# The MLP of a decoder block as two sweeps: up-projection by seven products of halves with factors parked in DRAM, then down-projection with two row blocks per accumulation

## The chip, the cores and the metric

The kernel is one program on one core of a Trainium2 chip. A core has TensorE (PE, matrix products from SBUF into PSUM), VectorE (DVE), ScalarE (ACT), GpSimd (POOL) and SyncE (SP), which here issues the DMA transfers between DRAM and SBUF. Each engine works through its own queue in order; semaphores tie the queues together. The metric is the device time of one execution in microseconds (us), as the median of several runs. One execution was recorded by the hardware profiler, and all rows below come from it.

## The reference, cut to what matters

The layer holds an attention-like part (gated DeltaNet beside differential attention), its output projection, and an MLP. The change is in the MLP alone.

```python
S, D_MODEL, D_FF = 512, 2048, 8192
h = h + einsum("bse,ed->bsd", mix, w_o)
u = rms_norm(h, mlp_norm)
hid = square(relu(einsum("bsd,df->bsf", u, w_up)))     # w_up 2048 x 8192
h = h + einsum("bsf,fd->bsd", hid, w_down)             # w_down 8192 x 2048
return rms_norm(h, final_norm)
```

All of it is float32. The kernel makes each float32 product from three products in a shorter format (float32r): every operand is written as hi + lo, and hi·hi, hi·lo and lo·hi are added up in PSUM.

## The kernel before, in words

Weights come in units of 128 partitions x 1024 numbers (512 KB). `load_w` (L160) issues a unit's DMA on SP's queue, each behind the load before it. `parts` splits the unit `raw`: ACT copies it to `hi` (L172), DVE subtracts to get `lo` (L174). `hi` and `lo` have three buffers each (`BUFS`), so unit n can be split only once TensorE is done with unit n−3. `raw` has six buffers. A scheduler decides the order in which the instructions of the streams stand in each engine's queue.

The hidden layer is cut into 16 blocks of 512 columns. Three things are done for a block.

- **Up** (`up_steps`, `cols_steps`): plain products, four groups of 128 hidden columns, each over 16 k tiles of 128, all 512 tokens wide: 4 x 16 x 3 = 192 matmuls of 512 columns. Its weights are the units with tag `x`. ACT makes the squared ReLU. Block 0 (`up_first`) is done first, in the time in which the transposed and normalised u is still being made (`to_feature_major`, `split_rows`, L189).
- **Left factors** (`seven_steps`, `two`): a block's 512 x 512 activations are taken as 2 x 2 blocks a11, a12, a21, a22 of 256 x 256. Winograd's form of Strassen's scheme needs seven left factors: a11, a12, a22 and the sums s1 = a21 + a22, s2 = s1 − a11, s4 = a12 − s2, s3 = a11 − a21. DVE makes the sums (L786 to L797); each factor is split by ACT (L774) and DVE (L775) and stays in SBUF.
- **Down** (`block_steps`, `product`): for each of two pairs p of column groups, the four quarters of the weights b11, b12, b21, b22 (two k tiles by 512 columns) are combined on DVE to t1 to t4 (L838, L844, L852, L858) in place of the loaded quarters, and seven products of 12 matmuls of 512 columns are added by DVE to the rows `h` in SBUF, 16 additions of 128 x 512 (L824 and L826). There are 15 blocks x 2 pairs in this form; block 15 is done by plain products (`plain_steps`).

The down of block b is woven with the up of the blocks after it: after every other product comes a step of up. A plain block costs 8 products of quarters where the scheme has 7.

Of the kernel before, what the change touches and what calls it, by code (L numbers as in the profile page):

```python
# [31 lines left out]
def hybrid_block(ctx: ExitStack, tc: tile.TileContext, x, attn_norm, w_in, conv_w, a_log, dt_bias,  # L32
# [601 lines left out]
    def attn_cols(hd, st):  # L634
        """Columns of q and k of both maps of a head."""
# [20 lines left out]
    def attention(hd, st, vt, keep=None):  # L656
        """The sweep over the query blocks, each in three stages that follow one another a step apart."""
# [110 lines left out]
    def half_tile():  # L768
        """[feature, token half, k tile, token]: two k tiles of a factor."""
        return big("p", [P, 2, 2, 256], nm="hf")  # L770

    def two(src):
        z = big("w", [P, 2, 2, 256], F32R, nm="op")
        A.activation(z[:, 0], src, AF.Copy)  # L774
        V.tensor_sub(z[:, 1], src, z[:, 0].bitcast(F32))  # L775
        return z[:, 0], z[:, 1]

    def seven_steps(left, f):
        """The seven left factors from a block's two K halves, in the order of their use."""
# [6 lines left out]
        V.tensor_add(s1, a21, a22)  # L786
        yield
        f["s1"] = two(s1)
        V.tensor_sub(s2, s1, a11)
        yield  # L790
        f["s2"] = two(s2)
        s4 = s1
        V.tensor_sub(s4, a12, s2)
        yield
        f["s4"] = two(s4)
        s3 = s2
        V.tensor_sub(s3, a11, a21)  # L797
        yield
        f["s3"] = two(s3)
        yield  # L800
        f["a22"] = two(a22)
        yield

    def product(bank, fac, wts, first, last_):
        (ah, al), (bh, bl) = fac, wts
        for k in range(2):
            for t in range(2):
                st = slice(t * P, (t + 1) * P)
                T.matmul(bank[t], lhsT=ah[:, k, st], rhs=bh[:, k, :], start=first and k == 0, stop=False, skip_group_check=True)  # L809
                T.matmul(bank[t], lhsT=ah[:, k, st], rhs=bl[:, k, :], start=False, stop=False, skip_group_check=True)  # L810
# [265 lines left out]
```

## Time and profile before

| what | value |
|---|---|
| median of 3 runs | 2296.26 us (2293.96 to 2299.38) |
| span of the profiled execution | 2291.4 us |
| TensorE busy in the span | 2251.6 us, 10,713 matmuls and transposes |
| VectorE busy | 1499.7 us |
| ScalarE busy | 896.7 us |
| GpSimd busy | 55.8 us |
| DMA, mean over the span | 107 GB/s |

The profiled execution lasted a span of 2291.4 us between its first and last instruction, 4.9 us under the median of the runs; what lies around the span is in that difference. The busy time of an engine is the time in which at least one of its instructions ran. Matmuls are pipelined, so their durations in a row are longer than the distance between their starts. Times in the rows count from the start of the span: about 0 to 960 us is the attention half with its projections, 962 to 1010 us the first block of up, 1010 to 2220 us the woven up and down, and the rest the last block and the final norm.

### The profile page before, as it was taken

Reading aid. Unit: us, or ns where it says so; the run is one execution under the profiler, and the core shown is the slowest. Engines: PE = TensorE matmul, PEld = TensorE weight load, DVE = VectorE, ACT = ScalarE, POOL = GpSimd, SP = SyncE. Lnnn points to the kernel's source line nnn. Section 1 sums busy time; section 2 is a strip of 40 time slices with the busy share of each in tenths; the row PEclk is TensorE's granted clock in tenths of the full one; section 3 lists DMA queues with packets and bytes.
Section 4 is the critical chain, followed back from the end, with each engine's and each line's share of the span. In section 5 each row is a group of like instructions: output and inputs, shape, how many; then the busy total and the mean of one; then the engine's idle time right before and its main releaser. Section 6 shows DMA issues by size and latency. Waiting matters only on the chain.

```text
span 2291.4 us, 27556 instructions
## 1 busy us (share of the span) xinstructions
PE 2251.6 (98%) x10713; PEld 1870.3 (82%) x10713; DVE 1499.7 (65%) x2296; ACT 896.7 (39%) x1468; POOL 55.8 (2%) x85
## 2 busy tenths in 40 slices
PE   6999999999999999999999999999999999999998
PEld 6988778778888788788888888888888888888886
DVE  5356977863255533446777787677777778767776
ACT  5233344432344532443443344334334334334443
POOL 0001101100000000000000000000000000000000
PEclk9999999999999999999999999999999999999999
DMA  5444333334232424332433324233233332323332
GB/s 175 126 115 119 106 108 95 115 88 113 83 88 91 153 83 133 107 101 83 129 92 102 110 83 129 92 120 92 85 127 92 108 104 86 126 92 119 92 129 93
DMA packets 286440, 245.49 MB, mean 107 GB/s; under 512 B 17211, under 2 KB 229478, under 8 KB 286310
## 3 DMA queue, kind: packets, MB, share of 16 engines
q1 hardware_dynamic: 285632, 243.45, 34.7%
q8 instruction: 84, 1.38, 0.2%
q10 hardware_dynamic: 678, 0.28, 0.1%
q14 instruction: 46, 0.38, 0.1%
HBM read 232.66 MB, written 11.03 MB: 106 GB/s over the span
## 4 chain that ended last, share of the span: by engine, by line
PE 93%; DVE 5%; ACT 1%; DMA 1%; issue 0%; POOL 0%; ACTq 0%; POOLq 0%; DVEq 0%
PE s L230 9%; PE s L231 9%; PE s L229 9%; PE acc L810 6%; PE acc L809 6%; PE acc L811 6%; PE acc L229 5%; PE acc L230 5%; PE acc L231 5%; PE acc L245 3%; PE acc L246 3%; PE acc L247 3%; PE s L810 2%; PE s L809 2%; PE s L811 2%; PE s L246 2%
## 5 line engine op out<-in xcount | busy, mean ns | idle before, releaser
L174 DVE TENSOR_TENSOR lo<-raw,hi 128x1024 fp32r<-128x1024 f32 (+2 forms) x370 | 444.1, 1201 | 427.3 <-ACT hi L172 416.6
L172 ACT ACTIVATE hi<-raw 128x1024 fp32r<-128x1024 f32 (+2 forms) x370 | 384.7, 1041 | 682.2 <-PE acc L230 135.8
L229 PE MATMUL s<-u,hi 128*128 128x512 f32 x960 | 373.4, 389 | 0.0
L230 PE MATMUL s<-u,hi 128*128 128x512 f32 x960 | 373.4, 389 | 0.0
L231 PE MATMUL s<-u,lo 128*128 128x512 f32 x960 | 373.4, 389 | 0.0
L174 DVE TENSOR_TENSOR lo<-x,hi 128x1024 fp32r<-128x1024 f32 x120 | 146.8, 1223 | 181.1 <-ACT hi L172 181.1
L229 PE MATMUL acc<-u,hi 128*128 128x512 f32 x640 | 259.8, 406 | 0.5 <-DVE dvl L653 0.5
L230 PE MATMUL acc<-u,hi 128*128 128x512 f32 x640 | 251.5, 393 | 0.0
L172 ACT ACTIVATE hi<-x 128x1024 fp32r<-128x1024 f32 x120 | 127.5, 1062 | 315.1 <-PE s L230 226.3
L231 PE MATMUL acc<-u,lo 128*128 128x512 f32 x640 | 250.2, 391 | 0.0
L810 PE MATMUL acc<-lo,op 128*128 128x512 f32 x600 | 233.4, 389 | 0.0
L811 PE MATMUL acc<-hi,op 128*128 128x512 f32 x600 | 233.4, 389 | 0.0
L809 PE MATMUL acc<-hi,op 128*128 128x512 f32 x600 | 233.1, 389 | 0.0
L824 DVE TENSOR_TENSOR h<-acc,h 128x512 f32<-128x512 f32 x360 | 232.2, 685 | 0.6 <-PE acc L811 0.5
L229 PEld LDWEIGHTS s<-u,hi 128*128 128x128 f32 x960 | 180.2, 188 | 37.4
L231 PEld LDWEIGHTS s<-u,lo 128*128 128x128 f32 x960 | 180.2, 188 | 37.4
L230 PEld LDWEIGHTS s<-u,hi 128*128 128x128 f32 x960 | 180.2, 188 | 37.4
L245 PE MATMUL acc<-hi,u 128*128 128x512 f32 (+2 forms) x384 | 145.3, 378 | 3.0 <-DVE cv L391 1.8
L247 PE MATMUL acc<-hi,u 128*128 128x512 f32 (+2 forms) x384 | 140.8, 367 | 0.0
L231 PEld LDWEIGHTS acc<-u,lo 128*128 128x128 f32 x640 | 120.2, 188 | 25.2
L229 PEld LDWEIGHTS acc<-u,hi 128*128 128x128 f32 x640 | 120.4, 188 | 24.9 <-issue 0.9
L246 PE MATMUL acc<-lo,u 128*128 128x512 f32 (+2 forms) x384 | 140.4, 366 | 0.0
(261 smaller groups left out, 3230.9 us busy)
## 6 DMA issues: line engine op xcount, KB each, us to landing
raw<-in_w_down_dram SPq DMA_DIRECT2D x128, 512.0 KB, 5.4
x<-in_w_up_dram SPq DMA_DIRECT2D x120, 512.0 KB, 4.6
raw<-in_w_in_dram SPq DMA_DIRECT2D x96, 512.0 KB, 3.9
raw<-in_w_o_dram SPq DMA_DIRECT2D x32, 512.0 KB, 4.2
raw<-in_w_in_dram SPq DMA_DIRECT2D x16, 384.0 KB, 3.9
x<-in_x_dram SPq DMA_DIRECT2D x8, 512.0 KB, 5.0
raw<-in_x_dram SPq DMA_DIRECT2D x8, 512.0 KB, 4.0
raw<-in_w_up_dram SPq DMA_DIRECT2D x8, 512.0 KB, 3.9
```

The source lines that it names most:

```text
L172: A.activation(hi, raw, AF.Copy)
L174: floor["lo"] = V.tensor_sub(lo, raw, hi.bitcast(F32))
L229: T.matmul(po, lhsT=hi[:, j, :], rhs=ah, start=k == 0, stop=False)
L230: T.matmul(po, lhsT=hi[:, j, :], rhs=al, start=False, stop=False)
L231: T.matmul(po, lhsT=lo[:, j, :], rhs=ah, start=False, stop=k == KD - 1)
L245: T.matmul(o, lhsT=ah[:, st], rhs=bh, start=k == 0, stop=False)
L246: T.matmul(o, lhsT=ah[:, st], rhs=bl, start=False, stop=False)
L247: T.matmul(o, lhsT=al[:, st], rhs=bh, start=False, stop=k == KD - 1)
L809: T.matmul(bank[t], lhsT=ah[:, k, st], rhs=bh[:, k, :], start=first and k == 0, stop=False, skip_group_check=True)
L810: T.matmul(bank[t], lhsT=ah[:, k, st], rhs=bl[:, k, :], start=False, stop=False, skip_group_check=True)
L811: T.matmul(bank[t], lhsT=al[:, k, st], rhs=bh[:, k, :], start=False, stop=last_ and k == 1, skip_group_check=True)
L824: V.tensor_add(dst, bank[t], dst)
```

## The change

The MLP runs as two sweeps instead of one woven stream.

**Up sweep.** Block 0 stays plain. For blocks 1 to 15 the up-projection is done by the seven products as well, with the transposed u as one factor: 2 x 2 blocks of 1024 k by 256 tokens. `u_factors` makes the seven factors of u once and keeps them in SBUF; for this u is first put together again as hi + lo, 16 additions of 128 x 512 on GpSimd (`uf`). Per block `up_steps` loads eight weight units of four k tiles x 256 columns, makes t1 to t4 on DVE (eight subtractions of 128 x 1024, L1081), and `up_product` runs seven products of two units, 24 matmuls of 256 columns per unit. DVE adds the products up from PSUM (L1109, L1122, L1128, L1129), GpSimd makes c22 (L1131). While block b is computed, `seven_steps` makes the left factors of block b − 1: the four sums now on GpSimd (L790, L793, L798, L803), the splits on ACT (L771) and DVE (L772), and `keep` stores each factor to DRAM (`fscr`, L781) on SP's queue. The rows h are stored to DRAM (`hscr`) to make room, and come back (`hb`) for the second sweep.

**Down sweep.** Fourteen blocks go in seven groups of two: the product of one factor pair of both blocks is accumulated in the same PSUM banks, so the 16 additions to the rows come once for two blocks. `recall` (L818) loads the left factors from DRAM. t1 and t2 are made on DVE, t3 and t4 on GpSimd (L854), two subtractions of 128 x 1024 for each. Block 14 is a group by itself, block 15 plain. Its left factors are stored at the beginning of the sweep. Buffers for `raw` are nine instead of six. The scratch memory of the DMA machinery is cut to 1024 bytes, and comments are removed.

```diff
-    BUFS = {"p": 10, "x": 2, "w": 8, "m": 2, "u": 16, "raw": 6, "hi": 3, "lo": 3}
+    BUFS = {"p": 10, "x": 2, "w": 8, "m": 2, "u": 16, "raw": 9, "hi": 3, "lo": 3}
...
+    def keep(b, name, src):
+        z = pair_of(src, "w")
+        fscr[b, name] = dp.tile([P, 1024], F32, name=f"f_{name}_{b}")
+        nc.sync.dma_start(out=fscr[b, name], in_=z.bitcast(F32).rearrange("p a k s -> p (a k s)"))
...
+        G.tensor_add(s1, a21, a22)
+        keep(b, "a11", a11)
+        yield
+        G.tensor_sub(s2, s1, a11)
+        keep(b, "s1", s1)
...
+    def recall(b, name):
+        z = big("w" if name in ("a12", "a22") else "u", [P, 2, 2, 256], F32R, nm="fac")
+        with tc.issue_after(last_load[0].ins):
+            last_load[0] = nc.sync.dma_start(out=z.bitcast(F32).rearrange("p a k s -> p (a k s)"), in_=fscr[b, name])
+        return z[:, 0], z[:, 1]
...
+    def product(bank, facs, wts, first, last_):
+        for n, ((ah, al), raw) in enumerate(zip(facs, wts)):
+            bh, bl = parts(raw, 2)
...
+        diff(V, t1, b12, b11)
+        Z = [acc(), acc()]
+        product(Z, fa, t1, True, False)
+        add(Z, 1, p + 2)
...
+        diff(G, t3, b22, b12)
+        product(X, factor("s3"), t3, False, True)
...
-    def up_steps(b, j, left):
-        z = half_tile()
-        for k in range(2):
-            po = sps()
-            yield from cols_steps(po, w_up[0], (4 * b + 2 * j + k) * P, uT, tag="x")
...
+        G.tensor_tensor(uf[k // 8][k % 8 // 2][:, k % 2], uh[k][:, :, 0, :].bitcast(F32), uh[k][:, :, 1, :].bitcast(F32), op=ALU.add)
...
-    for b in range(NBLK - 2):
-        down = block_steps(facs[b], w_down[0], 512 * b, h)
...
+    def u_factors():
+        for q in range(4):
+            xa, xb = uf[0][q], uf[1][q]
+            a11, a21, a12, a22 = xa[:, :, 0, :], xa[:, :, 1, :], xb[:, :, 0, :], xb[:, :, 1, :]
+            z = big("m", [P, 2, 2, 256], nm="s12")
+            s1, s2 = z[:, 0], z[:, 1]
...
+            V.tensor_add(s1, a21, a22)
+            put("s1", s1, "p")
...
+    def up_product(bank, name, wts, first, last_):
+        for n, raw in enumerate(wts):
+            bh, bl = parts(raw, 4)
+            for j in range(4):
+                k = 4 * n + j
+                ah, al = fu[name][k][:, 0, :], fu[name][k][:, 1, :]
+                for c in range(2):
+                    dst, st = bank[:, c * 256:(c + 1) * 256], slice(c * P, (c + 1) * P)
+                    head, tail = first and k == 0 and c == 0, last_ and k == 7
+                    T.matmul(dst, lhsT=bh[:, j, st], rhs=ah, start=head, stop=False, skip_group_check=True)
+                    T.matmul(dst, lhsT=bh[:, j, st], rhs=al, start=False, stop=False, skip_group_check=True)
+                    T.matmul(dst, lhsT=bl[:, j, st], rhs=ah, start=False, stop=tail, skip_group_check=True)
+    def up_steps(b, left):
+        def quarter(i, j):
+            c0 = 512 * b + 256 * j
+            return [load_w(w_up[0, 1024 * i + 512 * n:1024 * i + 512 * n + 512, c0:c0 + 256].rearrange("(k p) n -> p k n", p=P), [P, 4, 256])
+                    for n in range(2)]
...
+        diff(t2, b22, t1)
+        bB = acc()
+        up_product(bB, "s2", t2, True, False)
+        V.tensor_add(u2, bB, x1)
+        yield
...
+        diff(t3, b22, b12)
+        up_product(bB, "s3", t3, False, True)
+        V.tensor_add(u3, bB, x1)
+        V.tensor_sub(c21, u3, bD)
+        squared_relu(c21)
+        G.tensor_add(c22, u3, p5)
+        squared_relu(c22)
+        yield
...
+    left = up_first()
+    for b in range(1, NBLK):
+        fac, nxt = seven_steps(b - 1, left), []
+        for _ in up_steps(b, nxt):
+            next(fac, None)
+        run(fac)
+        left = nxt
+    last_fac = four_steps(NBLK - 1, left)
...
+    groups = [[b, b + 1] for b in range(0, NBLK - 2, 2)] + [[NBLK - 2]]
+    for g in groups:
+        f = {}
         for p in range(2):
-            ups = up(b + 1, 1) if p == 0 else up(b + 2, 0)
-            fac = seven_steps(lefts[b + 1], facs[b + 1]) if p == 1 else iter(())
-            for i in range(7):
-                next(down)
-                next(fac, None)
-                if i % 2 == 0:
-                    next(ups, None)
-            run(ups)
-    down = block_steps(facs[NBLK - 2], w_down[0], 512 * (NBLK - 2), h)
-    ups = up(NBLK - 1, 1)
-    for i in range(7):
-        next(down)
-        if i % 2 == 0:
-            next(ups, None)
-    run(ups)
-    lft = lefts[NBLK - 1]
-    fac = [[two(lft[j][:, i]) for i in range(2)] for j in range(2)]
+            down = block_steps(g, f, p, w_down[0], h)
+            if g is groups[0]:
+                rows_back((p, p + 2))
+            if g is groups[-1] and p == 1:
+                break
+            for _ in down:
+                next(last_fac, None)
```

VectorE's queue at one place of the up and down weave before: `raw` units of w_down in place of which t1 to t4 are made, `x` units of w_up, and additions of products (`acc`, `s` are PSUM) to rows `h`.

```order
L838 TENSOR_TENSOR raw_10296<-raw_10298,raw_10296 128x1024
L824 TENSOR_TENSOR h_7383<-s_10303,h_7383 128x512
L852 TENSOR_TENSOR raw_10298<-raw_10300,raw_10298 128x1024
L174 TENSOR_TENSOR lo_10378<-raw_10296,hi_10377 128x1024
L844 TENSOR_TENSOR raw_10296<-raw_10300,raw_10296 128x1024
L858 TENSOR_TENSOR raw_10294<-raw_10296,raw_10294 128x1024
L174 TENSOR_TENSOR lo_10398<-x_10395,hi_10397 128x1024
L824 TENSOR_TENSOR h_7379<-acc_10354,h_7379 128x512
L824 TENSOR_TENSOR h_7383<-acc_10355,h_7383 128x512
L174 TENSOR_TENSOR lo_10427<-raw_10296,hi_10426 128x1024
```

VectorE's queue at the border of two blocks in the up sweep after the change; `e` and `hf` hold sums of products and the block's activations, `s_1509` the sums for the left factors, `op` the factors' lo halves.

```order
L174 TENSOR_TENSOR lo_9515<-raw_9483,hi_9514 128x1024
L1081 TENSOR_TENSOR raw_9550<-raw_9620,raw_9550 128x1024
L1128 TENSOR_TENSOR e_9001<-acc_9147,e_9000 128x512
L1081 TENSOR_TENSOR raw_9483<-raw_9552,raw_9483 128x1024
L1129 TENSOR_TENSOR hf_8998<-e_9001,acc_9280 128x512
L174 TENSOR_TENSOR lo_9558<-raw_9481,hi_9557 128x1024
L174 TENSOR_TENSOR lo_9586<-raw_9483,hi_9585 128x1024
L1081 TENSOR_TENSOR raw_9481<-raw_9620,raw_9481 128x1024
L1081 TENSOR_TENSOR raw_9483<-raw_9622,raw_9483 128x1024
L772 TENSOR_TENSOR op_9545<-hf_8998,op_9545 128x512
L772 TENSOR_TENSOR op_9615<-s_1509_9543,op_9615 128x512
L174 TENSOR_TENSOR lo_9628<-raw_9481,hi_9627 128x1024
```

The additions of rows are gone here; between the `lo` of a product's first unit and the `lo` of the next product's first unit stand the subtractions of weights (L1081), two sums with PSUM, and splits of the factors of the block before.

GpSimd's queue at the same place; before the change it had no instruction in the whole woven part.

```order
L1131 TENSOR_TENSOR hf_8999<-e_9001,e_9000 128x512
L790 TENSOR_TENSOR s_1509_9543<-hf_8998,hf_8999 128x512
L793 TENSOR_TENSOR s_1509_9543<-s_1509_9543,hf_8998 128x512
L798 TENSOR_TENSOR s_1509_9543<-hf_8999,s_1509_9543 128x512
L803 TENSOR_TENSOR s_1509_9543<-hf_8998 128x512
```

The five 128 x 512 sums of a block now stand here: c22 first, which reads what VectorE's L1128 wrote, then s1, s2, s4 and s3.

VectorE's queue at the start of an iteration of the down sweep after the change: `raw_16888` and `raw_16890` are the b11 units of two blocks, `raw_16932` and `raw_16934` b12, `raw_16978` and `raw_16980` b22.

```order
L854 TENSOR_TENSOR raw_16888<-raw_16932,raw_16888 128x1024
L174 TENSOR_TENSOR lo_16911<-raw_16890,hi_16910 128x1024
L850 TENSOR_TENSOR hb_15707<-hb_15707,s_16848 128x512
L850 TENSOR_TENSOR hb_15707<-hb_15707,s_16849 128x512
L854 TENSOR_TENSOR raw_16890<-raw_16934,raw_16890 128x1024
L174 TENSOR_TENSOR lo_16941<-raw_16888,hi_16940 128x1024
L854 TENSOR_TENSOR raw_16888<-raw_16978,raw_16888 128x1024
L174 TENSOR_TENSOR lo_16957<-raw_16890,hi_16956 128x1024
L848 TENSOR_TENSOR hb_15704<-acc_16892,hb_15704 128x512
L848 TENSOR_TENSOR hb_15704<-acc_16893,hb_15704 128x512
L854 TENSOR_TENSOR raw_16890<-raw_16980,raw_16890 128x1024
L174 TENSOR_TENSOR lo_16985<-raw_16888,hi_16984 128x1024
```

Each `parts` now comes twice, for two blocks, and t1 and t2 alternate with the splits; t3 and t4 are not in the queue any more.

GpSimd's queue in the same iteration and the first of the next.

```order
L854 TENSOR_TENSOR raw_16932<-raw_16978,raw_16932 128x1024
L854 TENSOR_TENSOR raw_16934<-raw_16980,raw_16934 128x1024
L854 TENSOR_TENSOR raw_17102<-raw_16888,raw_17102 128x1024
L854 TENSOR_TENSOR raw_17104<-raw_16890,raw_17104 128x1024
L854 TENSOR_TENSOR raw_17224<-raw_17266,raw_17224 128x1024
```

The first two rows are t3 of the two blocks, over b12, the next two t4, over b21, and the last is t3 of the iteration after.

SP's queue where the up sweep ends and the down sweep begins; `f_a_15`'s stores take factors of the last block, the others load factors and weights for the first group.

```order
L781 DMA f_a_15_15763<-op_15760 128x1024
L160 DMA raw_15769<-in_w_down_dram 128x2x512
L160 DMA raw_15771<-in_w_down_dram 128x2x512
L781 DMA f_a_15_15814<-op_15811 128x1024
L818 DMA fac_15816<-f_s_0_8729 128x1024
L818 DMA fac_15818<-f_s_1_9208 128x1024
L160 DMA raw_15820<-in_w_down_dram 128x2x512
L160 DMA raw_15822<-in_w_down_dram 128x2x512
L781 DMA f_a_15_15863<-op_15860 128x1024
L818 DMA fac_15865<-f_s_0_8861 128x1024
L818 DMA fac_15867<-f_s_1_9340 128x1024
L781 DMA f_a_15_15906<-op_15903 128x1024
```

Loads of weights for the first group stand behind stores that wait for the last block's activations.

## Rows read from the trace of the kernel before

**Rows 1.** Page, part 1: span, busy time and instructions of each engine.

```profile
span 2291.4 us, 27556 instructions
...
PE 2251.6 (98%) x10713; PEld 1870.3 (82%) x10713; DVE 1499.7 (65%) x2296; ACT 896.7 (39%) x1468; POOL 55.8 (2%) x85
```

**Rows 2.** Busy time by stretch; a bracket counts instructions, the last numbers are clock, DMA, GB/s.

```profile
962.00:1010.00 48.00, 46.70 (x234) 38.37 (x235) 23.60 (x34) 23.28 (x35) 0.68 (x1) 1.00 0.20 55
1010.00:2220.00 1210.00, 1210.00 (x5340) 1001.93 (x5339) 907.25 (x1074) 476.80 (x560) 0.00 (x0) 1.00 0.34 105
```

**Rows 3.** TensorE in order of time, 256 columns wide: start, duration, engine, line, operation.

```profile
674.72 0.28 PE L707 MATMUL s<-dvh,at 128*128 128x256 f32 x1
...
675.67 0.28 PE L709 MATMUL s<-dvh,at 128*128 128x256 f32 x1
675.79 0.40 PE L229 MATMUL acc<-u,hi 128*128 128x512 f32 x1
```

**Rows 4.** TensorE in order of time, 272 columns wide, a stream without gaps.

```profile
99.83 0.29 PE L247 MATMUL acc<-hi,u 128*128 128x272 f32 x1
...
101.35 0.28 PE L247 MATMUL acc<-hi,u 128*128 128x272 f32 x1
```

**Rows 5.** Groups by line and shape, VectorE and then ScalarE, 1100 to 2200 us.

```profile
L174 DVE TENSOR_TENSOR lo<-raw,hi 128x1024 fp32r<-128x1024 f32 x189 | 231.2, 1223 | 115.5 <-ACT hi L172 115.5
L824 DVE TENSOR_TENSOR h<-acc,h 128x512 f32<-128x512 f32 x323 | 208.2, 685 | 0.0
...
L172 ACT ACTIVATE hi<-raw 128x1024 fp32r<-128x1024 f32 x189 | 199.8, 1057 | 307.6 <-PE s L230 112.1 <-PE acc L811 104.1 <-DVE raw L838 65.0
```

**Rows 6.** VectorE in order of time, inside the up and down weave of one block.

```profile
1500.33 1.23 DVE L174 TENSOR_TENSOR lo<-raw,hi 128x1024 fp32r<-128x1024 f32 x1
1501.47 0.69 DVE L775 TENSOR_TENSOR op<-s,op 128x512 fp32r<-128x512 f32 x1
1502.08 0.68 DVE L793 TENSOR_TENSOR s<-hf,s 128x512 f32<-128x512 f32 x1
1502.68 1.22 DVE L174 TENSOR_TENSOR lo<-raw,hi 128x1024 fp32r<-128x1024 f32 x1
```

**Rows 7.** GpSimd's groups, and one of its instructions with no other work beside it.

```profile
L436 POOL TENSOR_SCALAR_AFFINE_SELECT pT<-pT 128x1024 f32<-128x1024 f32 x4 | 5.2, 1297 | 5.8 <-ACT pT L432 5.8
...
442.75 1.10 POOL L436 TENSOR_SCALAR_AFFINE_SELECT pT<-pT 128x1024 f32<-128x1024 f32 x1 [1.25 <-ACT pT L432]
```

**Rows 8.** GpSimd and VectorE at the same moments, in order of time.

```profile
178.20 1.23 POOL L434 TENSOR_SCALAR_AFFINE_SELECT dm<-dm 128x1024 f32<-128x1024 f32 x1 [156.71 <-ACT dm L432]
181.14 1.90 POOL L436 TENSOR_SCALAR_AFFINE_SELECT pT<-pT 128x1024 f32<-128x1024 f32 x1 [1.71 <-ACT pT L432]
...
178.32 1.19 DVE L431 TENSOR_SCALAR pT<-pT,gc 128x128 f32<-128x128 f32 x1
...
L431 DVE TENSOR_SCALAR pT<-pT,gc x32: 275/285/1207, 176.9 to 440.4; 128x128 f32<-128x128 f32 x32
...
180.87 1.22 DVE L174 TENSOR_TENSOR lo<-raw,hi 128x1024 fp32r<-128x1024 f32 x1
```

**Rows 9.** VectorE in order of time where the MLP begins.

```profile
965.68 2.73 DVE L189 SCALAR_TENSOR_TENSOR u<-s,vec,u 128x512 fp32r<-128x512 f32 x4 [0.43 <-ACT u L188]
...
972.75 2.73 DVE L189 SCALAR_TENSOR_TENSOR u<-s,vec,u 128x512 fp32r<-128x512 f32 x4 [0.80 <-ACT u L188]
976.04 1.22 DVE L174 TENSOR_TENSOR lo<-raw,hi 128x1024 fp32r<-128x1024 f32 x1 [0.57 <-ACT hi L172]
```

**Rows 10.** DMA issues (KB of one, median us to landing), and the busiest stretch.

```profile
raw<-in_w_down_dram SPq DMA_DIRECT2D x128, 512.0 KB, 5.4
x<-in_w_up_dram SPq DMA_DIRECT2D x120, 512.0 KB, 4.6
...
105.00:108.00 3.00, 3.00 (x26) 3.00 (x25) 0.72 (x1) 0.66 (x1) 0.00 (x0) 1.00 0.98 261
```

More of the change, by code (lines that the diff above doesn't have):

```diff
@@ L785, in seven_steps @@
         s1, s2 = z[:, 0], z[:, 1]
[L786 removed]
+        G.tensor_add(s1, a21, a22)
+        keep(b, "a11", a11)
         yield
[L788 to L789 removed]
+        G.tensor_sub(s2, s1, a11)
+        keep(b, "s1", s1)
         yield
[L791 to L793 removed]
+        keep(b, "s2", s2)
         yield
[L795 to L797 removed]
+        G.tensor_sub(s1, a12, s2)
@@ L798, in seven_steps @@
+        keep(b, "a12", a12)
         yield
-        f["s3"] = two(s3)
+        keep(b, "s4", s1)
         yield
-        f["a22"] = two(a22)
+        G.tensor_sub(s2, a11, a21)
+        keep(b, "a22", a22)
         yield
-    def product(bank, fac, wts, first, last_):
-        (ah, al), (bh, bl) = fac, wts
-        for k in range(2):
-            for t in range(2):
-                st = slice(t * P, (t + 1) * P)
-                T.matmul(bank[t], lhsT=ah[:, k, st], rhs=bh[:, k, :], start=first and k == 0, stop=False, skip_group_check=True)
-                T.matmul(bank[t], lhsT=ah[:, k, st], rhs=bl[:, k, :], start=False, stop=False, skip_group_check=True)
-                T.matmul(bank[t], lhsT=al[:, k, st], rhs=bh[:, k, :], start=False, stop=last_ and k == 1, skip_group_check=True)
@@ new lines, in seven_steps, with four_steps @@
+        keep(b, "s3", s2)
+        yield
+    def four_steps(b, left):
+        for j in range(2):
+            for i in range(2):
+                keep(b, f"a{i + 1}{j + 1}", left[j][:, i])
+                yield
[4 more added lines that the diff above has]
+        return z[:, 0], z[:, 1]
@@ new lines, in block_steps, with factor, add, diff @@
+    def block_steps(bs, f, p, w, rows):
+        def quarter(i, j):
+            c0 = 1024 * j + 512 * p
+            return [load_w(w[512 * b + 256 * i:512 * b + 256 * i + 256, c0:c0 + 512].rearrange("(k p) n -> p k n", p=P), [P, 2, 512])
+                    for b in bs]
+        def factor(name):
+            if name not in f:
+                f[name] = [recall(b, name) for b in bs]
+            return f[name]
+        def add(bank, half, cg, op=ALU.add):
+            for t in range(2):
+                dst = rows[2 * half + t][cg]
+                if op == ALU.add:
+                    V.tensor_add(dst, bank[t], dst)
+                else:
+                    V.tensor_sub(dst, dst, bank[t])
+        def diff(E, out, a, b):
+            for o, x1, x2 in zip(out, a, b):
+                E.tensor_sub(o, x1, x2)
+        fa = factor("a11")
+        b11 = quarter(0, 0)
+        X = [acc(), acc()]
+        product(X, fa, b11, True, False)
+        add(X, 0, p)
+        yield
+        fa = factor("s1")
+        b12 = quarter(0, 1)
+        t1 = b11
+        diff(V, t1, b12, b11)
+        Z = [acc(), acc()]
+        product(Z, fa, t1, True, False)
+        add(Z, 1, p + 2)
+        yield
+        fa = factor("s2")
+        b22 = quarter(1, 1)
+        t2 = t1
+        diff(V, t2, b22, t1)
+        product(X, fa, t2, False, False)
+        add(X, 0, p + 2)
+        yield
+        product(Z, factor("s4"), b22, False, True)
+        add(Z, 0, p + 2)
+        yield
+        t3 = b12
+        diff(G, t3, b22, b12)
+        product(X, factor("s3"), t3, False, True)
+        add(X, 1, p)
+        add(X, 1, p + 2)
+        yield
+        fa = factor("a12")
+        b21 = quarter(1, 0)
+        Y = [bank(), bank()]
+        product(Y, fa, b21, True, True)
+        add(Y, 0, p)
+        yield
+        t4 = b21
+        diff(G, t4, t2, b21)
+        Y = [bank(), bank()]
+        product(Y, factor("a22"), t4, True, True)
+        add(Y, 1, p, ALU.subtract)
+        yield
@@ L954, in up_first @@
                     T.matmul(po[c], lhsT=lo[:, j, st], rhs=ah, start=False, stop=k == KD - 1)
+        floor.clear()
+        run(u_factors())
+        left = []
         for j in range(2):
@@ new lines, in hybrid_block, with rows_back @@
+    left = up_first()
[6 more added lines that the diff above has]
+    last_fac = four_steps(NBLK - 1, left)
+    hb = []
+    for i in range(8):
+        z = big("p", [P, 2, 512], nm="hb")
+        hb.append(z)
+    h = [[hb[2 * cg + t // 2][:, t % 2, :] for cg in range(4)] for t in range(NT)]
+    def rows_back(cgs):
+        for cg in cgs:
+            for i in range(2):
+                nc.sync.dma_start(out=hb[2 * cg + i], in_=hscr[2 * cg + i])
```

199 lines of the change are left out of this document (120 added, 79 removed).

## The prediction

> **What bounds the kernel now.** First the page's busy times: TensorE is busy for 2251.6 of 2291.4 us [rows 1]. Then the busy time by stretch [rows 2]: from 1010 to 2220 us, which is the woven up and down, TensorE is busy in all of 1210.00 us at granted clock 1.00 (the 2.4 GHz level), VectorE in 907 us (75%), ScalarE in 477, GpSimd in none, the DMA engines at 0.34 of their time and 105 GB/s. So only fewer or shorter matmuls save time there, and whatever makes TensorE wait costs in full. The 5340 matmuls of this stretch give 1210.00/5340 = 226.6 ns for one of 512 columns.
>
> The profiled span lies 4.9 us under the median of the runs, 2296.3; I add my sum to the median. A change under 0.2% (4.6 us) is about what a measurement of this kernel can't tell from none.
>
> **What is removed and added on TensorE.** Up by plain products was 15 blocks x 192 = 2,880 matmuls of 512 columns: 2,880 x 0.2266 = 652.6 us. The seven products of halves are 15 x 7 products x 2 units x 24 = 5,040 matmuls of 256 columns. Before has few of these. Nine of them in a row start within 675.79 − 674.72 = 1.07 us, 119 ns each [rows 3]; a longer stream, 272 wide, takes 1.52 us for twelve, 127 ns each, or 119.2 for 256 columns [rows 4]. That is 5% above half of 226.6. 5,040 x 0.1192 = 600.8 us, **a gain of 52 us** (53 at 118.9 ns, 48 at 120). Down keeps its 2,520 seven-product matmuls and block 15's, up of block 0 stays, so this is the whole gain on TensorE.
>
> **Whether the other engines keep up on average.** VectorE: a 128x1024 subtraction lasts 1.22 us [rows 5] but the next instruction starts 1.14 us after it (1500.33 to 1501.47), and 0.60 us after one of 512 (1502.08 to 1502.68) [rows 6]; I count starts. Per block of the up sweep: 14 `lo` and 8 weight subtractions at 1.135, 4 sums with PSUM and 7 factor splits at 0.60, together 31.6 us, against TensorE's 336 x 0.1192 = 40.1. Per iteration of the down sweep (two blocks, one pair of column groups): 14 `lo`, 4 subtractions, 16 additions, 30.0 us, against 168 x 0.2266 = 38.1. ScalarE needs 14 x 1.06 plus small ones [rows 5], less than VectorE. Halving the additions of rows is worth nothing by itself, since VectorE is not the bound.
>
> **GpSimd.** It gets five sums of 128x512 per up block, four subtractions of 128x1024 per down iteration and 16 sums at the start. Before shows no such instruction. The nearest row is a select of 128x1024 with one input: 1.10 us when alone, 1.30 in the mean [rows 7]. With two inputs, the lower bound is 1.1 (both read at once) and the upper 2.2 (one after the other); for 512 half of that. I take 2.0 and 1.0, near the upper end, as there is twice as much to read as in the row.
>
> What matters is that VectorE and GpSimd hold each other up. A VectorE instruction that otherwise takes 0.28 us took 1.19 us (178.32 to 179.51) while GpSimd ran from 178.20 to 179.43; and a GpSimd select took 1.90 us instead of 1.10 when it met a `lo` subtraction that ran from 180.87 to 182.09: 1.90 is the rest of that `lo`, 0.95, and a little less than a select of its own [rows 8]. So one waits for the other's whole instruction. The Trainium skill, "SBUF — State Buffer", section "Who interferes with whom", says the same of a VectorE instruction with two SBUF inputs beside a GpSimd instruction that reads SBUF, and exempts VectorE instructions with an operand from PSUM; the rows agree on the first. The skill's "GPSIMD Engine Reference", section 3.1, has 4497 ns for an addition of 2048 float32, which gives an estimate of 2.25 us for 1024; by it the sum below would be 28 us instead of 17.
>
> By this, `lo`, the weight subtractions and the splits are held for the length of a GpSimd instruction; additions from PSUM are not.
>
> **Up sweep, one block border.** TensorE needs a new unit each 24 x 0.1192 = 2.86 us, and with three buffers for `hi` and `lo` a unit can be split only when the third one before it is consumed. So VectorE can be 8.6 us ahead at most. From its `lo` of a block's unit 1 to that of unit 4 stand 12 instructions (the queue's rows shown: eight of 1024, four of 512): 8 x 1.135 + 4 x 0.60 = 11.5 us. It starts 1.1 us before TensorE begins the block, so it is done at 10.5, or 11.0 with 0.5 us of waiting for a `hi` that stands behind the ReLU of c22. Unit 4 is needed at 4 x 2.86 = 11.4. There is 0.4 us of slack, and three GpSimd sums (c22, s1, s2) fall into this stretch. At 1.0 us each, 0.6 of one beneath a PSUM sum, they hold VectorE 2.4 us: TensorE waits 2.0 us. At 1.1 it is 2.3; at 0.55 it is 0.6 (1.65 less the 0.6 beneath is 1.05, less the slack). Later in the block VectorE catches up. 15 borders x 2.0 = **+30 us** (+9 to +35).
>
> **Down sweep, one iteration.** A unit is due each 12 x 0.2266 = 2.72 us. t3 of the first block can run from 1.9 us before the iteration begins and holds the `lo` of unit 1 (L174's first row in the piece shown); t3 of the second can run only when t1 of the second is made, at 4.7 to 4.9 us, and holds t2 and thus `lo` 3 (due 8.16) and `lo` 4 (10.88). Walking the queue with 1.1 for a subtraction no unit is late; with 2.0, 1.6 us in all; with 2.2, 2.0 us. t4 comes where VectorE has PSUM additions and delays nothing. 14 iterations x 1.6 = **+22 us** (0 to +28).
>
> **Once only.** *Start:* VectorE's first sum of u's factors needs GpSimd's tenth sum and stands ahead of the `lo` of the second unit, which before started at 976.04 [rows 9]. GpSimd's sums follow u's tiles, of which the first four are made from 965.68 on and the ninth to twelfth from 972.75 on; ten sums of 1.0 in a row from 966.4, when the first tile is done, end past 976; with the sums of u_factors (some 20 us on VectorE, in a stretch of 48 in which it was busy for 23.6 [rows 2]) I put +5 (0 to +11). *Transition:* loads of b12 and b22 stand on SP behind the store of block 15's first factor. A load takes 5.4 us to land [rows 10], so `lo` of unit 2 is ready at about 10.7 instead of 5.4: +7 with some of it covered by the units ahead (0 to +12). *Block 14 alone:* 7 `lo`, 2 subtractions, 16 additions and two held subtractions are 10.2 + 9.6 + 4.0 = 23.8 us for 84 x 0.2266 = 19.0 of TensorE: +5 (0 to +10). Together **+17**.
>
> **DMA.** The extra 115 MB are: seven factors of 512 KB stored per block, loaded once, and the rows. Up moves 7.5 MB per 40 us, 188 GB/s; down 15 MB (two iterations) per 76 us, 197 GB/s. Before reached 261 GB/s at a share of 0.98 [rows 10], so this is three quarters of what the engines can do. With nine buffers for `raw`, loads run up to eight units ahead, over 20 us, and I price it at nothing; without that cover see the third rival.
>
> **Sum.** −52 + 30 + 22 + 17 = +17: **about 2313 us**, slightly slower. With all upper bounds of GpSimd: −52 + 35 + 28 + 17 = +28.
>
> **Rivals.** (1) *GpSimd is fast*, 1.1 us for 1024 and 0.55 for 512, or hardly holds VectorE: −52 + 9 + 0 + 12 = −31, 2265; with no delay at all 2244. For it: the one row of 1.10. Against it: two inputs. This decides the sign: the point of balance is near 1.5 us for 1024 and 0.75 for 512. Chance 0.36. (2) *No change within 4.6 us*, the costs between the two: 0.12. (3) *The loads are late*: with transfers at 200 GB/s a unit that lands 5 us later than now stalls each iteration of down, 14 x 5 = +70 on top of −52 + 30 + 17, about 2361. For it: the share of three quarters and stores and loads in one queue; against it: nine buffers. Chance 0.08. (4) *256-wide matmuls fall to the weight load's pace*: excluded by the 272-wide stream [rows 4]; 0.01. My forecast's own case, delays of the size above, has 0.43.
>
> **Range.** The forecast's case spans 2301 to 2335, the first rival 2244 to 2291. Leaving out a tenth at each end gives 2256 to 2345. Faster 0.36, same 0.12, slower 0.52.
>
> **What would show it.** TensorE's up matmuls at 119 ns in their stream, and about 2 us idle per up block, ended by `lo` (L174) with VectorE subtractions of over 2 us beside L790 to L803 or L1131; in the down sweep subtractions L854 on GpSimd of about 2.0 us and TensorE idle of 1.6 us near units 3 and 4. Wrong: GpSimd's groups near 1.1 us for 1024, TensorE without gaps in either sweep, or gaps that end with a DMA.

## The result, and the profile after

The changed kernel takes 2350.9 us (2346.0 to 2355.2) against 2296.26: ratio 1.0241, interval 1.0223 to 1.0258. Slower, as forecast, but by 54.6 us instead of 17, and 6 us above the range. The profiled execution has a span of 2353.5 us, 62.1 longer than before's; it is the longest of the four runs, 4.3 us over their median, so the stretches below add up to more than 54.6. The page's first part [rows 1 for before]:

```profile
span 2353.5 us, 33224 instructions
...
PE 2247.8 (96%) x12873; PEld 1959.1 (83%) x12873; DVE 1697.8 (72%) x2258; ACT 998.4 (42%) x1608; POOL 382.6 (16%) x236
```

TensorE's busy time is hardly shorter, though it does its up-projection in fewer products. The busy time by stretch (start, up sweep, down sweep; TensorE, its weight loads, VectorE, ScalarE, GpSimd; in brackets the instructions; then TensorE's granted clock, DMA share and GB/s) [rows 2]:

```profile
962.00:1026.00 64.00, 56.29 (x265) 45.59 (x264) 55.06 (x78) 36.23 (x61) 23.56 (x18) 0.95 0.25 76
1026.00:1679.50 653.50, 626.11 (x5041) 623.27 (x5040) 546.00 (x490) 347.68 (x467) 145.04 (x74) 0.97 0.54 185
1679.50:2320.00 640.50, 606.65 (x2604) 488.92 (x2604) 564.82 (x553) 235.56 (x237) 160.54 (x62) 0.99 0.55 197
```

Three things are to be seen: TensorE is no longer busy all the time (626 of 653 us, 607 of 640), its granted clock is 0.95, 0.97 and 0.99 where it was 1.00, and GpSimd works in both sweeps. What TensorE waited for in the up sweep (total us, times, longest):

```profile
PE acc L1070 <- DVE lo L174: 27.4, 14, 2.0
```

and of the down sweep:

```profile
PE acc L829 <- DVE lo L174: 25.6, 30, 1.7
PE acc L828 <- ACT hi L172: 6.5, 2, 4.4
```

So 14 waits for `lo` at the 14 borders of blocks, all near 2.0 us, and about two in each iteration of down. One border of the up sweep, first VectorE, then GpSimd, in order of time (start, duration) [rows 6 and 7 for what they take alone]:

```profile
1113.03 0.68 DVE L1129 TENSOR_TENSOR hf<-e,acc 128x512 f32<-128x512 f32 x1
1113.63 1.72 DVE L174 TENSOR_TENSOR lo<-raw,hi 128x1024 fp32r<-128x1024 f32 x1
1115.91 1.22 DVE L174 TENSOR_TENSOR lo<-raw,hi 128x1024 fp32r<-128x1024 f32 x1 [0.57 <-ACT hi L172]
1117.06 3.45 DVE L1081 TENSOR_TENSOR raw<-raw,raw 128x1024 f32<-128x1024 f32 x2
1120.43 1.78 DVE L772 TENSOR_TENSOR op<-hf,op 128x512 fp32r<-128x512 f32 x1
```

```profile
1112.12 2.14 POOL L1131 TENSOR_TENSOR hf<-e,e 128x512 f32<-128x512 f32 x1 [20.28 <-DVE e L1128]
1117.52 1.91 POOL L790 TENSOR_TENSOR s<-hf,hf 128x512 f32<-128x512 f32 x1 [3.25 <-ACT hf L1085]
1119.51 2.16 POOL L793 TENSOR_TENSOR s<-s,hf 128x512 f32<-128x512 f32 x1
```

While c22 (L1131) runs, the `lo` at 1113.63 takes 1.72 us instead of 1.22, but L1129, which has one operand in PSUM, its usual 0.68. While s1 and s2 run (L790, L793), two weight subtractions take 3.45 us where alone they took about 2.3, and a split takes 1.78 instead of 0.69. GpSimd's own 1.91 and 2.16 contain the time in which it was held. VectorE lost 2.7 us at this border (0.5, 1.1 and 1.1), and TensorE waited 1.95. Its rows there:

```profile
1121.77 0.28 PE L1069 MATMUL acc<-us,hi 128*128 128x256 f32 x1
1124.01 0.39 PE L1070 MATMUL acc<-us,lo 128*128 128x256 f32 x1 [1.95 <-DVE lo L174]
...
1124.64 0.42 PE L1068 MATMUL acc<-us,hi 128*128 128x256 f32 x1
1124.86 0.41 PE L1069 MATMUL acc<-us,hi 128*128 128x256 f32 x1
1125.07 0.41 PE L1070 MATMUL acc<-us,lo 128*128 128x256 f32 x1
```

The wait ends at 1124.01, and from 1124.64 on matmuls start 0.213 us apart instead of 0.120: sixteen of them. The stretch's granted clock:

```profile
1124.70:1127.50 2.80, 2.80 (x15) 2.80 (x15) 2.80 (x3) 0.00 (x0) 0.39 (x1) 0.50 0.34 132
```

That is the lower of the two levels (0.50, 1.2 GHz), and it costs another 16 x 0.093 = 1.5 us. Counted from the first matmul of a block to that of the next, 12 borders cost 3.97 us over 336 matmuls at 0.1192. Two borders with the same wait (behind the matmuls at 1297.83 and 1516.46) were not followed by it and cost 2.48, so the lower clock is 1.5 us of the 3.97; the clock behind the first of them:

```profile
1300.20:1303.00 2.80, 2.80 (x24) 2.80 (x25) 2.80 (x2) 0.11 (x1) 0.96 (x1) 1.00 0.56 217
```

In the down sweep GpSimd's t3 does the same. GpSimd, then VectorE, at the start of an iteration:

```profile
1728.06 2.39 POOL L854 TENSOR_TENSOR raw<-raw,raw 128x1024 f32<-128x1024 f32 x1 [6.22 <-DVE raw L854]
1733.95 3.32 POOL L854 TENSOR_TENSOR raw<-raw,raw 128x1024 f32<-128x1024 f32 x1 [3.49 <-DVE raw L854]
```

```profile
1728.16 3.37 DVE L174 TENSOR_TENSOR lo<-raw,hi 128x1024 fp32r<-128x1024 f32 x1 [0.23 <-ACT hi L172]
...
1735.04 3.31 DVE L854 TENSOR_TENSOR raw<-raw,raw 128x1024 f32<-128x1024 f32 x1
```

A `lo` takes 3.37 us and a subtraction 3.31, 2.1 us too long each. TensorE loses 2.47 us in 12 iterations and 1.32 in one, in two waits; in the 12 the longer is 1.34 to 1.37 us. Behind it the matmuls go on 0.227 us apart, and the granted clock of the 13 iterations is 1.00:

```profile
1739.54 0.50 PE L829 MATMUL acc<-lo,fac 128*128 128x512 f32 x1 [1.37 <-DVE lo L174]
1739.88 0.39 PE L830 MATMUL acc<-hi,fac 128*128 128x512 f32 x1
1740.11 0.39 PE L828 MATMUL acc<-hi,fac 128*128 128x512 f32 x1
...
1729.60:2255.00 525.40, 503.17 (x2184) 407.65 (x2183) 467.66 (x443) 191.84 (x183) 136.98 (x53) 1.00 0.55 198
```

GpSimd's 128x1024 subtraction by itself (least, median, most, in ns) and two of its 128x512 groups (busy us, mean ns):

```profile
L854 POOL TENSOR_TENSOR raw<-raw,raw x60: 2387/2400/3340, 1694.1 to 2301.6; 128x1024 f32<-128x1024 f32 x60
```

```profile
L793 POOL TENSOR_TENSOR s<-s,hf 128x512 f32<-128x512 f32 x15 | 32.4, 2160 | 1.2
...
L803 POOL TENSOR_TENSOR s<-hf 128x512 f32<-128x512 f32 x15 | 22.0, 1468 | 140.1 <-DVE op L772 140.1
```

Alone it takes 2.39 us for 1024 columns, and 1.29 for 512 (the least of L803).

### The profile page after: what moved, and what is told of

The parts are those of the page before. It is cut to its first block, busy times and chain, and to the rows that moved or that the text cites. A ratio compares the mean times of both kernels' runs of the same rounds, so it can differ in the third digit from the quotient of the medians.

```text
span 2353.5 us, 33224 instructions
## 1 busy us (share of the span) xinstructions
PE 2247.8 (96%) x12873; PEld 1959.1 (83%) x12873; DVE 1697.8 (72%) x2258; ACT 998.4 (42%) x1608; POOL 382.6 (16%) x236
## 4 chain that ended last, share of the span: by engine, by line
PE 67%; DVE 15%; issue 9%; ACT 3%; DMA 3%; POOL 2%; SPq 0%; DVEq 0%; POOLq 0%; ACTq 0%
DVE lo L174 6%; PE acc L229 5%; PE acc L230 5%; PE acc L231 5%; PE acc L829 3%; PE acc L830 3%; PE acc L245 3%; PE acc L247 3%; PE acc L246 3%; PE acc L828 3%; PE acc L1070 3%; PE acc L1069 3%; PE acc L1068 3%; PE s L1069 3%; PE s L1068 3%
## 5 line engine op out<-in xcount | busy, mean ns | idle before, releaser
L174 DVE TENSOR_TENSOR lo<-raw,hi 128x1024 fp32r<-128x1024 f32 (+2 forms) x580 | 773.0, 1336 | 446.0 <-ACT hi L172 433.7
L172 ACT ACTIVATE hi<-raw 128x1024 fp32r<-128x1024 f32 (+2 forms) x580 | 602.4, 1046 | 987.4 <-PE acc L830 146.8
L829 PE MATMUL acc<-lo,fac 128*128 128x512 f32 x600 | 239.5, 399 | 25.6 <-DVE lo L174 25.6
L828 PE MATMUL acc<-hi,fac 128*128 128x512 f32 x600 | 234.9, 393 | 6.5 <-ACT hi L172 6.5
L830 PE MATMUL acc<-hi,fac 128*128 128x512 f32 x600 | 235.8, 393 | 0.0
L854 POOL TENSOR_TENSOR raw<-raw,raw 128x1024 f32<-128x1024 f32 x60 | 158.7, 2646 | 463.9 <-DVE lo L174 119.1
L1081 DVE TENSOR_TENSOR raw<-raw,raw 128x1024 f32<-128x1024 f32 x120 | 161.5, 1356 | 1.2
L229 PEld LDWEIGHTS acc<-u,hi 128*128 128x128 f32 x640 | 120.8, 189 | 25.1 <-issue 0.9
L230 PEld LDWEIGHTS acc<-u,hi 128*128 128x128 f32 x640 | 120.8, 189 | 23.8 <-issue 1.4
L1070 PE MATMUL s<-us,lo 128*128 128x256 f32 x480 | 135.8, 283 | 0.0
L1070 PE MATMUL s<-uh,lo 128*128 128x256 f32 x480 | 135.8, 283 | 0.0
L1068 PE MATMUL acc<-uh,hi 128*128 128x256 f32 x480 | 135.8, 283 | 0.0
L1069 PE MATMUL acc<-uh,hi 128*128 128x256 f32 x480 | 135.8, 283 | 0.0
```

Of the source, the lines that this page charges most:

```text
L172: A.activation(hi, raw, AF.Copy)
L174: floor["lo"] = V.tensor_sub(lo, raw, hi.bitcast(F32))
L229: T.matmul(po, lhsT=hi[:, j, :], rhs=ah, start=k == 0, stop=False)
L230: T.matmul(po, lhsT=hi[:, j, :], rhs=al, start=False, stop=False)
L830: T.matmul(bank[t], lhsT=al[:, k, st], rhs=bh[:, k, :], start=False, stop=tail, skip_group_check=True)
L1068: T.matmul(dst, lhsT=bh[:, j, st], rhs=ah, start=head, stop=False, skip_group_check=True)
```

## The experiments

All are told with the median of their runs, and in brackets the ratio to before and its 95% interval; before took 2293.5 to 2294.2 in these comparisons. The stages are measured between matmuls of the profiled execution: in the changed kernel start 62.5 us (54.3 before), up 653.6, first iteration of down 50.2, the 13 after it 525.8, rest 89.3.

**t3 and t4 on VectorE.**

```diff
-        diff(G, t3, b22, b12)
+        diff(V, t3, b22, b12)
-        diff(G, t4, t2, b21)
+        diff(V, t4, t2, b21)
```

> The two subtractions t3 and t4 of the down sweep move from GpSimd to VectorE; up sweep unchanged. Theory A (a GpSimd instruction and a VectorE instruction with two SBUF inputs hold each other up for the whole instruction): the 2.47 us lost in each of 13 iterations of the down sweep shrink to about 0.5, since VectorE then needs 34.5 of 38.1 us and its queue from lo of unit 1 to lo of unit 4 is 12.6 us long for the 12.3 us that it has; with a little from the last group about 28 us less, 2323 us. Rival B (VectorE is short of time, and GpSimd relieved it): 4.5 us more per iteration on VectorE, the losses stay or grow, 2351 or more. Rival C (late loads set the gaps): nothing changes, 2351.

2315.5 us (1.0098, 1.0083 to 1.0113). The 13 iterations take 497.0 us, 0.17 lost in each instead of 2.47. VectorE got 4.5 us more work per iteration and the waits went: theory A.

**All sums of the up sweep on VectorE.** `G.` becomes `V.` in L790, L793, L798, L803 and L1131.

> The five 128x512 sums per block of the up sweep (c22 and the four sums of the left factors) move from GpSimd to VectorE; down sweep unchanged. Theory A, with TensorE's clock as a second part (it falls to 1.2 GHz after a wait of 2.1 us and not after waits of 1.5): VectorE's queue from lo of unit 1 to lo of unit 4 becomes 13.3 us long, unit 4 is about 1 us late and no slow stretch follows, so a block loses 1 instead of 4 us: 14 x 3 = 42 less, 2309 us. Without the clock part the wait shrinks by 1 us only: 14 less, 2337. Rival B (VectorE is short of time): 3 us more work per block, a loss of 4 or more, 2351 or more.

2313.6 us (1.0087, 1.0072 to 1.0102). The loss per block is 0.93 us instead of 3.97; the waits for `lo` in the up sweep:

```profile
PE acc L1070 <- DVE lo L174: 5.7, 14, 0.4
```

**Both.**

> Both moves together: in both sweeps VectorE does all sums and subtractions, GpSimd none (it keeps the 16 sums at the start). Theory A: the two gains add up, 70 less, 2281 us, below the kernel before. Rival B: 2351 or more.

2277.1 us (0.9929, 0.9914 to 0.9944). The gains of the two moves were 35 and 37 us; together they give 74. This is the base of what follows.

**The factors' sums later, still on GpSimd.**

```diff
-        for _ in up_steps(b, nxt):
-            next(fac, None)
+        for i, _ in enumerate(up_steps(b, nxt)):
+            if i >= 2:
+                next(fac, None)
```

> The sums of the left factors stay on GpSimd but are begun two products later in each block of the up sweep; c22 stays where it is. Nothing else changes. Theory A: at the border of two blocks only c22 holds VectorE, for at most 0.7 us, so the wait falls to about 0.5 us and no slow stretch of TensorE follows; 14 x 3.4 = 48 less, and some of it is given back where the other sums now fall: 2305 to 2320 us. If not the place but the amount of GpSimd work costs the time, nothing changes, 2351.

2364.7 us (1.0308, 1.0291 to 1.0325): a miss. The edit did not do what it was meant to: most of the splits moved away from the border, but s1 and s2 still ran there on GpSimd (1114.96 to 1119.11 at one border), which had nothing else to do. A block lost 4.3 us, and the first iteration of down, behind factors that now came later, 16.9. It tells nothing of place against amount.

**s1 alone on VectorE.**

> The changed kernel with one sum of five (s1) moved from GpSimd to VectorE in the up sweep; down sweep unchanged. This halves the holding at the border of two blocks: TensorE's wait goes from 2.1 to about 1.5 us. Theory with TensorE's clock as a part of its own (it falls to 1.2 GHz after a wait of 2.1 us but not after 1.5): the loss per block falls from 4.0 to 1.5 to 1.8 us, 14 x 2.3 = 32 less, 2319. If the wait alone costs: 14 x 0.6 = 8 less, 2343.

2372.2 us (1.0339, 1.0324 to 1.0355): another miss, and the wait grew to 3.0 us. With s1 out of its queue GpSimd came to s4 (L798) earlier, 12.7 us behind the `lo` of unit 1 instead of 13.9. GpSimd and VectorE:

```profile
1118.59 2.11 POOL L798 TENSOR_TENSOR s<-hf,s 128x512 f32<-128x512 f32 x1 [1.29 <-DVE op L772]
```

```profile
1119.50 2.28 DVE L174 TENSOR_TENSOR lo<-raw,hi 128x1024 fp32r<-128x1024 f32 x1
```

The `lo` held here for 2.28 us is that of unit 4, the one TensorE waits for. So VectorE is held for as long as before at this border (0.5, 1.1 and 1.1 us) and has s1 itself, 0.6 us, in its queue besides: the holding moved to another place instead of shrinking.

**A shorter wait in the same order.** t2 covers 768 of 1024 columns; the rest of t2 is left out.

```diff
-        diff(t2, b22, t1)
+        diff([z[:, 0:768] for z in t2], [z[:, 0:768] for z in b22], [z[:, 0:768] for z in t1])
```

> The changed kernel in which the subtraction t2 of the up sweep covers 768 of its 1024 columns (the rest of t2 is left out, so the output differs). The order of the queues at the border of two blocks stays as it is, only two instructions of VectorE are 0.28 us shorter each, so TensorE's wait goes from 2.1 to about 1.5 us. Theory with TensorE's clock as a part of its own (it falls to 1.2 GHz after waits of 2.1 us and not after 1.5): the loss per block falls from 4.0 to about 1.5 us, 14 x 2.3 = 32 less, 2319. If only the wait itself costs: 14 x 0.6 = 8 less, 2343.

2327.1 us (1.0138, 1.0123 to 1.0153), the up sweep 628.3 us instead of 653.6. TensorE at a border:

```profile
1114.92 0.28 PE L1069 MATMUL acc<-us,hi 128*128 128x256 f32 x1
1116.63 0.39 PE L1070 MATMUL acc<-us,lo 128*128 128x256 f32 x1 [1.43 <-DVE lo L174]
1116.85 0.28 PE L1068 MATMUL acc<-us,hi 128*128 128x256 f32 x1
1116.97 0.28 PE L1069 MATMUL acc<-us,hi 128*128 128x256 f32 x1
```

The wait is 1.43 us, and the matmuls behind it go on at 0.12 us. All 14 borders cost 1.93 to 1.95 us. So 0.5 us less wait saved 2.0 at the 12 borders that had been followed by the low clock: the clock is a cost of its own.

**The start in another order** (on the kernel without GpSimd in the sweeps).

```diff
+            if u == 3:
+                mark.append(floor["lo"])
-            V.tensor_add(s1, a21, a22)
+            with tc.issue_after(mark[0].ins):
+                V.tensor_add(s1, a21, a22)
```

> The kernel without GpSimd in the two sweeps, and at the start VectorE's first sums of u's factors are put behind the lo of block 0's fourth weight unit, so that no lo waits for GpSimd's tenth sum. Theory: in the changed kernel the sum waited 3.6 us for GpSimd, the lo of the second unit came 7 us later than before and TensorE waited 4.6 us for it and then ran slowly; the stage took 62.2 us where it took 53.8 before. With the new order 4 to 8 of the 8.4 us come back: 2269 to 2273, against 2277 for its base. Rival: VectorE simply has too much to do in this stage (some 20 us of sums more); then the wait only moves to a later unit, 2275 to 2278.

2273.4 us (0.9906, 0.9892 to 0.9921). The start stage takes 55.9 us instead of 62.2; in the run's time 3.7 us of that are seen, hardly more than the intervals can tell apart.

**The last block's factors in the second group.** `next(last_fac, None)` only where `g is not groups[0]`.

> The kernel without GpSimd in the two sweeps, and the factors of the last block are made and stored during the second group of the down sweep instead of the first. Theory (the prediction's transition term): the loads of b12 and b22 no longer stand behind stores that wait for the last block's activations; the first iteration loses about 3 us instead of 10.2: 2270 against 2277 for its base. Rival: at this place the DMA engines are full (share 0.9 and more, loads taking 10 us to land), and the amount to be moved sets the loss; then nothing changes, 2277.

2273.9 us (0.9906, 0.9889 to 0.9922), 3.2 us under its base, again little beside the intervals. The first iteration takes 44.5 us instead of 48.3, the 13 after it 1.5 us more: under half of the first one's loss was the making and storing of these factors. The edit moves their splits on ScalarE and VectorE along with the stores, so it doesn't tell which of them cost the time. In the changed kernel VectorE's split of such a factor had waited 3.62 us for ScalarE, which stood behind c22, ahead of the first t1; the t2 after it waited 1.54 us for its load, and a load took 10.3 us to land around there, 1660 to 1712 us (KB, median us) [rows 10 for before]:

```profile
1684.68 1.29 DVE L772 TENSOR_TENSOR op<-hf,op 128x512 fp32r<-128x512 f32 x2 [3.62 <-ACT op L771]
1693.86 1.23 DVE L854 TENSOR_TENSOR raw<-raw,raw 128x1024 f32<-128x1024 f32 x1 [1.54 <-DMA raw<-in_w_down_dram]
...
raw<-in_w_down_dram SPq DMA_DIRECT2D x12, 512.0 KB, 10.3
```

**t4 back on GpSimd** (on the same base).

> The kernel without GpSimd in the two sweeps, but t4 of the down sweep is back on GpSimd (t3 stays on VectorE). The prediction said that t4 comes where VectorE has additions from PSUM and delays nothing: then 2277, as its base. Rival: whatever GpSimd does in this sweep holds VectorE where it hurts: up to 2 us in each of 14 iterations, 2290 to 2305.

2277.1 us (0.993, 0.9915 to 0.9945), as its base. It does hold VectorE, as GpSimd's row and VectorE's show, but no iteration loses by it (0.07 to 0.15 us each, no more than in the base), so VectorE is far enough ahead of TensorE there:

```profile
1745.79 2.40 POOL L854 TENSOR_TENSOR raw<-raw,raw 128x1024 f32<-128x1024 f32 x1 [32.20 <-DMA raw<-in_w_down_dram]
```

```profile
1747.15 2.12 DVE L174 TENSOR_TENSOR lo<-raw,hi 128x1024 fp32r<-128x1024 f32 x1 [1.49 <-ACT hi L172]
```

**One block per accumulation** (on the same base): `groups = [[b] for b in range(NBLK - 1)]`.

> The kernel without GpSimd in the two sweeps, with one block per accumulation in the down sweep instead of two, so that the 16 additions to the rows come for each block. The prediction held that halving the additions is worth nothing by itself. Theory: in a sweep that is only down, VectorE would need 7 lo, 4 subtractions and 16 additions, 22.1 us, for 84 matmuls that take 19.0; VectorE becomes the bound, 3.1 us lost in each of 28 products pairs that were paired before, some 87 more: 2364 against 2277 for its base. Rival: the prediction's sentence holds, 2277 to 2290.

2450.3 us (1.0677, 1.0659 to 1.0695), twice the loss expected. A pass is the seven products of one block for one pair of column groups. TensorE waits at each border of passes, here from 1700 to 2300 us, for a `hi` that in turn waits for VectorE's subtraction; VectorE is busy for 537.74 of these 600 us, TensorE for 508.47, and the granted clock is 0.93:

```profile
PE s L828 <- ACT hi L172: 74.0, 24, 3.1
ACT hi L172 <- DVE raw L854: 368.5, 79, 8.0
...
1700.00:2300.00 600.00, 508.47 (x1967) 383.71 (x1966) 537.74 (x635) 164.83 (x163) 0.00 (x0) 0.93 0.45 155
```

A pass takes 25.6 us where its 84 matmuls take 19.0, and more than the 22.1 worked out for VectorE: waits of 3.1 us and some shorter ones, and the low clock behind them.

**Both small gains, and the factors later on VectorE.** The last is the loop of the fourth experiment with `i >= 1`.

> The kernel without GpSimd in the two sweeps, with both the new order at the start and the later stores of the last block's factors. If the two gains (3.7 and 3.2 us) are of different places, they add up: 2270.

2268.3 us (0.9882, 0.9867 to 0.9896).

> The kernel before in this list, and the left factors' sums and splits, all on VectorE now, are begun one product later in each block of the up sweep. At the border of two blocks VectorE's queue from lo of unit 1 to lo of unit 4 is then 9.8 us long instead of 13.3, so the 0.93 us that TensorE still loses per block should go: 13 less, 2257, if the queue finds room for them later in the block (31.6 + 3 of 40 us are in use).

2258.1 us (0.9842, 0.9827 to 0.9857), the fastest. Its stretches:

```profile
962.00:1016.00 54.00, 52.98 (x268) 43.83 (x268) 51.31 (x68) 35.37 (x59) 25.19 (x17) 1.00 0.26 79
1020.00:1630.00 610.00, 609.10 (x5035) 606.56 (x5034) 528.89 (x573) 350.32 (x465) 0.00 (x0) 1.00 0.59 204
1630.00:2250.00 620.00, 611.25 (x2672) 500.68 (x2670) 565.44 (x632) 243.72 (x256) 1.90 (x4) 1.00 0.56 201
```

The up sweep has 120.0 us per 1000 matmuls of 256 columns and no waits. 14 blocks "lose" 0.27 us each against 0.1192: that is no wait, 0.120 us is the pace of this stream.

## Why the prediction was wrong

The direction and the mechanism of the waits were right, the size was not: the prediction gave a wait no price beyond its own length. By its own terms, for the profiled execution:

- **TensorE, −52:** −48. The stream runs at 120.0 ns a matmul, not 119.2.
- **Up borders, +30:** +49. The wait came out as worked out (27.4 us in 14 waits, 1.95 each against 2.0), in part by luck: a sum takes 1.29 us, not 1.0, and VectorE was held for 2.7 us, not 2.4, but the slack was 0.7 us (2.7 less 1.95), not 0.4. The step that failed is that "whatever makes TensorE wait costs in full" and no more: behind 12 of 14 waits TensorE ran at 1.2 GHz for sixteen matmuls or so. That added 12 x 1.5 = 18 us; some 3.5 more are lost around the waits (a border without the low clock costs 2.2 us at 0.120 us a matmul, for a wait of 1.95). No term and no rival held it, though before's clock of 1.00 was read off as if it were given. The two borders without it and the run with the shorter wait show it apart from the wait.
- **Down iterations, +22:** +31 in 13 iterations, 2.47 us lost in 12 of them where the prediction had 1.6; what it had wrong was the size of the GpSimd instruction. I took 2.0 us with an upper bound of 2.2; it is 2.39. The prediction's own walk gave 1.6 us for 2.0 and 2.0 for 2.2, which drawn on to 2.39 is an estimate of 2.4, and without GpSimd 0.15 us are still lost. The bound came from two passes over a one-input row, and left out that a second input may cost more than the first. The 4497 ns for an addition of 2048 float32 in the Trainium skill, "GPSIMD Engine Reference", section 3.1, give an estimate of 2.25, nearer than mine; the row decides at 2.39. In the step itself t3 held two instructions as said, and t4 cost nothing (shown by its own run).
- **Once only, +17 (5, 7, 5):** +8, +12 and +8. At the start the mechanism was as said, VectorE's first sum waited 3.6 us for GpSimd and was held itself:

```profile
981.58 1.74 DVE L1042 TENSOR_TENSOR s<-uf,uf 128x512 f32<-128x512 f32 x1 [3.60 <-POOL uf L994]
983.24 2.28 DVE L174 TENSOR_TENSOR lo<-raw,hi 128x1024 fp32r<-128x1024 f32 x1
```

The `lo` at 983.24 is that of the second unit, 7.2 us after before's [rows 9], of which 2.5 are that the MLP began later in this execution. TensorE waited 5.4 us for it, once more with the low clock after it:

```profile
PE acc L1012 <- DVE lo L174: 5.4, 1, 5.4
...
985.60:991.30 5.70, 5.70 (x14) 4.46 (x15) 5.70 (x6) 0.00 (x0) 4.97 (x4) 0.50 0.33 101
```

So the wait was near the +5; the other 2.8 us are fourteen matmuls at 0.427 us instead of 0.227. The first iteration of down shows the same: its waits of 4.4, 2.1, 0.5 and 0.5 us make 7.5, in size near the +7, and the low clock behind them adds some 3.5 (0.90 in the mean):

```profile
1679.40:1729.60 50.20, 42.72 (x171) 33.64 (x170) 38.03 (x39) 18.60 (x21) 14.22 (x6) 0.90 0.89 316
```

Its mechanism, stores ahead of loads, is shown only together with the splits, and for under half. Of block 14's +8, 3.4 us went with t3 and t4 on VectorE; the rest stays open.

- **DMA, 0:** right in the steady part. In the kernel without GpSimd 13 iterations took 496.8 us for 494.9 of matmuls, and the last kernel moved 204 and 201 GB/s in its two sweeps; TensorE did not wait at all from 1677 to 2167 us. Only in the first iteration loads were late. The 261 GB/s taken as the engines' limit was too low, as the row above shows (316 GB/s at a share of 0.89), and the extra traffic is 123 MB (368.5 against 245.5), not 115.
- **Halving the additions, "worth nothing by itself":** wrong. With single blocks the kernel without GpSimd is 173 us longer. The reason given, that VectorE is not the bound, held in the weave, where up's matmuls gave it time, not in a sweep of down alone.

The sum of the measured terms is −48 + 49 + 31 + 28 = 60 of 62.1 us. The rest is the part that the change leaves alone: it ended at 963.3 us here and at 960.8 before, and between 958 and 963 in all kernels here. Of the 43 us by which the terms exceed the forecast's 17, the low clock behind waits is some 24 (18, 2.8 and 3.5), the largest single part.

What stays open: the rest of the first iteration's loss (6 us even with the factors made later, the low clock behind one wait among them), and why two waits of 1.95 us were not followed by the low clock. The kernel with c22 or the later sums alone on GpSimd was not tried.

## What to carry to other kernels

Work moved to an idle GpSimd is not free where VectorE has instructions with two SBUF inputs: each holds the other for its whole length, and what counts is whether that falls where VectorE is ahead. Where TensorE is the bound at full clock, price a short wait at up to twice its length if the clock may fall behind it: here, against 0.120 us a matmul, a wait of 1.95 us cost 3.7, and one of 1.4 us cost 1.7. A rewrite that saves products can be right and still lose to where its helpers run: with the same products and the sums on VectorE it is 0.993 of before, and with three changes of order 0.984.

## What was not expected of the hardware

TensorE's granted clock fell to 0.50 (1.2 GHz) behind single waits of 1.95 us in a stream that was otherwise without gaps, in 12 of 14 cases, and was back 3.2 us later (matmuls 0.213 us apart from 1124.64 to 1127.85). Behind the waits of 1.4 us it did not, in 14 cases at 256 columns and in 12 at 512. A GpSimd subtraction of 128x1024 takes 2.39 us, twice VectorE's 1.22 and a little more than twice its own one-input select (1.10).
